# A decoder step bound by TensorE: a new opening for its first two units, side work moved between stages, and one group of heads fewer in plain form

## Chip, cores and metric

The kernel runs on one core of a Trainium2 chip. The metric is device microseconds of one execution. A core has five engines that run side by side, each in the order of its own queue: TensorE (PE; matmuls, with its weight loads shown as PEld), VectorE (DVE), ScalarE (ACT), GpSimd (POOL) and SyncE (SP). Here SP issues the loads and some stores, POOL issues most of the stores. Data lie in a fast memory of 128 partitions; matmuls write to a small second one (PSUM), and large arrays lie in DRAM.

## What is computed

One inference step of a two-layer decoder, on 1024 prompt tokens and 8 single decoded tokens, at width 2048, in float32:

```python
def pool_layer(x, prefix, pos, w_in, w_grp, scale, w_out, g_ln, b_ln):
    z = x @ w_in                                   # 2048 -> 4096: u and a gate
    u, gate = z[..., :D_POOL], z[..., D_POOL:]
    d, new_state = multiscale_pool(u, prefix, pos) # trailing means over 2, 4, 8, 16 tokens, minus u
    d = einsum('btgc,gce->btge', d, w_grp) * scale # four groups of 512 channels
    y = (d * silu(gate)) @ w_out
    return layer_norm(ALPHA * x + y, g_ln, b_ln), new_state

def shared_kv(h, pos, w_kv): ...                   # 4 key/value heads of 64, keys rotated

def attn_layer(x, pos, kb, vb, ...):
    z = x @ w_in                                   # 32 query heads of 64 (rotated) and a gate
    o = attn_core(q, kb, vb, q_pos, k_pos, sinks)  # causal window of 128, a learned sink per head
    y = (o * silu(gate)) @ w_out
    return layer_norm(ALPHA * x + y, g_ln, b_ln)
```

The first layer is `pool_layer`, then the keys and values are projected once, and the second layer is `attn_layer`. The outputs are both token streams and the new states and caches.

## The kernel before

Activations lie with channels on the partitions and tokens along the free axis. The tokens are worked in two chunks, 0 with 512 tokens and 1 with 520 (512 and the 8 decoded ones). The phases (PHASES, L50) follow each other in this order: `ai` (input projection, means, gate and group product of the first layer) for chunk 0 and then 1, `ao` (output projection and residual; its layer norm follows as side work) for 0 and 1, `bi` (keys, values, queries, gate and attention of the second layer) for 0 and 1, `bo` (its output projection) for 0 and 1.

**Products in float32 from three passes.** Each operand is split into a high part, a cast to the matmul's reduced format (on ScalarE: L502 for weights, L792 for activations), and a low part, the rest (a subtraction on DVE: L517 and L801). A product is three matmuls: high by high, high by low, low by high. So every piece of weights of 512 KB, once loaded, costs a cast and a subtraction before TensorE can use it up.

**Plain and Strassen form.** Most phases use a Strassen scheme of seven products (`seven`, L593): two output tiles of 128 channels at half the tokens, seven products of 8 x 3 = 24 matmuls with 256 or 260 columns (L681 to L683). The scheme needs sums of weight blocks and of activation blocks. Sums of weights are made by `first_pair` (L333, additions at L347) where a pair of tiles is used first, and may be stored for chunk 1, which loads them through `next_pair` (L319). Sums of activations, four per pair of rows, are made by `t_ops` (L843 to L853) and stored to DRAM as `Td`. The first part of `ai` chunk 0 and the first part of `bi` chunk 0 run in plain form (PLAIN, L57): there a tile of 128 output channels is a `unit` (L695) of two half steps with 24 matmuls of 512 columns each (L709 to L711). In `bi` chunk 0 the plain part has the keys and values (four units) and the first three pairs of query and gate tiles; a pair is four units, two with queries and two with gates. A pair takes two query tiles and so four heads.

**Order of work.** Every engine runs in the order of the source (L83). A counter `i` goes up at each `end()` (L541): once for each Strassen product, four times for each plain unit. Work that hangs on a product is put on this counter with `self.at(n, ...)`, n ends later. `begin()` (L529) loads the weights some pieces ahead, makes their casts and low parts three or four ahead and hands out the next piece. Beside this stand generators of side work (layer norms in `ln_gen`, L935; sums for the next phase in `t_gen`, L856; sums of weights in `sum_gen`, L428). `end()` takes one step of the first generator each time `i` passes a multiple of `every`, if at least `room` buffers are free (L554). `ready` (L570) runs a generator to its end at once if the next phase's input still hangs on it. Buffers come from one pool of 54 (`Mem`, L137), oldest freed first; a buffer whose last reader or store isn't done makes the new user wait.

**The start** (`start`, L2131). It issues, in turn, a load of the first weights (512 KB), eight loads of activation tiles (512 KB each, two rows of 128 channels by 512 tokens), with two more weight loads between them, and three small tables. Then come the casts and low parts in the order of need. The first unit uses all eight activation tiles one after the other; the next three units of the phase use them again. Four DVE groups (`t_first`, L748), placed at ends 3, 5, 7 and 9, make activation sums for the Strassen part.

**The means** (`pool_tile` and `pool_tail`, L1038 to L1105). After each unit ScalarE copies the result out (L1190); one end later DVE adds shifted copies (L1064), scales (L1085), and one end after that `rest` splits the result: a cast on ScalarE and the low part on DVE (`split`, L270 to L272) at the same end.

**Side work around the attention.** During `ao` chunk 1 the layer norm of chunk 0 runs, with `every` 2 and no sums for the Strassen part (its last argument is None, L2212). During the plain part of `bi` chunk 0, with `every` 1, run the layer norm of chunk 1 (with its sums), then `t_gen` for chunk 0, which loads the normalised rows again, makes the sums and stores them; ten additional steps are placed at ends 3, 5, ..., 21 (L2223). Beside them `sum_gen("wob")` may begin parts from end 4 to end 12. After a plain query unit the rotation (L1679, L1787) is put four ends after the unit's result is out, and TensorE's scores (L1817) one end later.

Of the kernel before, what the change touches and what calls it, by code (L numbers as in the profile page):

```python
# [9 lines left out]
F32 = mybir.dt.float32  # L10
# [37 lines left out]
N_CST = K_MP + P + 1  # L48

PHASES = (  # L50
    ("ai", 0, (0, 1)), ("ai", 0, (1, 8)), ("ai", 1, (0, 8)), ("ao", 0, None), ("ao", 1, None), ("bi", 0, (0, 3)),
    ("bi", 0, (3, 8)), ("bi", 1, (0, 8)), ("bo", 0, None), ("bo", 1, None),
)
PHASE_OF = {"x": "ai", "g": "ao", "h": "bi", "o": "bo"}
INPUT_OF = {k: x for x, k in PHASE_OF.items()}
# [133 lines left out]
class Kern:  # L189
# [185 lines left out]
    def build_stream(self):  # L375
        io = self.io
        w = []
        for kind, c, part in PHASES:
# [4 lines left out]
            if kind == "ai":  # L383
                for n in range(*part):
                    g, gates = divmod(n, 2)
                    for q in (8 * gates + 2 * g, 8 * gates + 2 * g + 1):
                        if n:
                            w += pr("wia", q)
                        elif c == 0:
                            w += self.bare_pair("wia", q)  # L390
                        else:
                            f = self.first_pair("wia", q, False)
                            w += [f[i] for i in ORDER7]
                    for h in range(2 if gates else 0):
                        w.append(self.lone(io["wg"][g][:, h * 1024 : (h + 1) * 1024]))
# [299 lines left out]
    def unit(self, done):  # L695
# [3 lines left out]
        for par in range(2):  # L699
            w = self.begin()  # L700
            wh, wl = (s.r for s in w)
            for k in range(8):
# [16 lines left out]
                if k in (3, 7):  # L719
                    self.end()  # L720


    def x_begin(self, n):

# [351 lines left out]
    def pool_tail(self, c, i, g, w, U, s, T, ext, dd, bufs, Us, work, add):  # L1076
        nc = self.nc
        for x in work:
            add(*x)
        if c == 0:  # L1080
            o = K_MP + g * NST
            nc.vector.tensor_mul(
                s[:, NST : NST + w - 1], s[:, NST : NST + w - 1], self.cst[:, o : o + w - 1]
            )
        nc.vector.scalar_tensor_tensor(  # L1085
            s[:, NST : NST + TP], s[:, NST : NST + TP], 1.0 / w, U[:, NST : NST + TP],
            op0=ALU.mult, op1=ALU.subtract,
        )
# [83 lines left out]
    def phase_ai(self, c, parts, nxt):  # L1172
# [5 lines left out]
        def means(g, end):  # L1178
            ext = es = None
            if T > TP:  # L1180
                es = self.mem.half(T)
                ext = es.a[:, :512].rearrange("p (i b w) -> p i b w", i=4, b=NDEC)
                nc.sync.dma_start(ext, io["st"][:, 4 * g : 4 * g + 4])
            dd = self.dd = {}
            for i in range(4):
                if not self.strassen:

                    def done(ps, i=i):
                        U = self.mem.full(NST + T)
                        nc.scalar.copy(U.a[:, NST : NST + T], ps[:])  # L1190
# [940 lines left out]
    def start(self):  # L2131
# [8 lines left out]
        self.load_to(1)  # L2140
        for n in range(8):
            self.x_load()
            if n in (3, 5):
                self.load_to(n // 2 + 1)
# [3 lines left out]
        self.prep_to(1)  # L2148
        for n in range(8):
            self.x_make()  # L2150
            if n == 3:
                self.prep_to(2)
# [7 lines left out]
    def run(self):  # L2160
# [15 lines left out]
        for n, (kind, c, part) in enumerate(PHASES):  # L2176
# [212 lines left out]
```

## Time and profile before

| | us |
|---|---|
| median of 3 runs | 2325.74 |
| lowest and highest | 2324.58, 2327.02 |
| the profiled execution | 2326.46 |
| its span, first to last instruction | 2324.7 |
| TensorE busy | 2290.2 |
| VectorE busy | 1935.0 |
| ScalarE busy | 1381.8 |
| GpSimd busy | 191.7 |

The times are those of whole executions; the profile shows one of them, and times in it count from the span's start. A row of the view of groups gives the line, the engine, the operation, output and input tiles with their shape, a count, then busy time, mean duration in ns, and the idle time of the engine just before with what ended it. A row of the timeline gives start, duration, and in brackets the idle time before it and its releaser. A row of the view of waits reads: who waited, for whom, total us, times, longest. A row of windows gives a stretch, its length, the busy time (and instructions) of PE, PEld, DVE, ACT and POOL, the clock that the throttle granted, the mean busy share of the 16 DMA engines, and GB/s. Matmuls and DVE operations overlap their neighbours, so the distance between two starts is less than a duration.

### The profile page before, as it was taken

The numbers are of one execution on the slowest core, as the hardware profiler recorded it, in microseconds if no ns is written. First come the engines' busy times: TensorE is split into PE (matmuls) and PEld (weight loads), VectorE is DVE, ScalarE is ACT, GpSimd is POOL, SyncE is SP. The second block draws the span as 40 slices with busy tenths as digits, with TensorE's granted clock in tenths as the row PEclk, the third lists the DMA queues.
The fourth block names the chain that finished last, engine by engine and source line by source line (L and its number), as shares of the span: only waits on it lengthen the run. The fifth ranks groups of instructions, "written<-read, shape, count | busy, mean of one in ns | idle before, by whom it ended". The sixth has DMA issues, their size and how long they took to land. (4 is left out here: it accounts for less than half of the span.)

```text
span 2324.7 us, 50174 instructions
## 1 busy us (share of the span) xinstructions
PE 2290.2 (99%) x20248; PEld 2208.9 (95%) x20248; DVE 1935.0 (83%) x2398; ACT 1381.8 (59%) x2531; POOL 191.7 (8%) x360
## 2 busy tenths in 40 slices
PE   8999999999999999999999999999999999999997
PEld 6999999999999999999778999999999999999997
DVE  7888889877878878878987888988987777898897
ACT  5554446544546556655466676785676678656565
POOL 0111110010000000000110111100000000000001
PEclk9999999999999999999999999999999999999999
DMA  6868679988889989898797667788586778799794
GB/s 247 280 252 304 234 243 333 322 299 302 303 306 317 338 284 336 321 350 310 236 349 256 220 224 254 256 306 259 178 262 225 252 233 284 254 368 363 266 345 157
DMA packets 247417, 652.50 MB, mean 281 GB/s; under 512 B 25328, under 2 KB 106128, under 8 KB 247184
## 3 DMA queue, kind: packets, MB, share of 16 engines
q1 hardware_dynamic: 205168, 496.81, 63.6%
q0 software_dynamic: 42016, 152.49, 17.0%
q8 instruction: 158, 2.59, 0.4%
q14 instruction: 75, 0.61, 0.1%
HBM read 466.68 MB, written 173.01 MB: 275 GB/s over the span
## 5 line engine op out<-in xcount | busy, mean ns | idle before, releaser
L681 PE MATMUL pD<-m,m 128*128 128x260 f32 (+1 forms) x4976 | 1408.7, 283 | 3.0 <-ACT pD L620 1.3
L683 PE MATMUL pD<-m,m 128*128 128x260 f32 (+1 forms) x4976 | 1402.2, 282 | 6.1 <-DVE m L517 5.7
L682 PE MATMUL pD<-m,m 128*128 128x260 f32 (+1 forms) x4976 | 1402.3, 282 | 0.0
L681 PEld LDWEIGHTS pD<-m,m 128*128 128x128 f32 x4976 | 936.6, 188 | 12.4 <-issue 6.0
L683 PEld LDWEIGHTS pD<-m,m 128*128 128x128 f32 x4976 | 937.7, 188 | 9.2 <-DVE m L517 9.2
L682 PEld LDWEIGHTS pD<-m,m 128*128 128x128 f32 x4976 | 937.0, 188 | 0.5
L517 DVE TENSOR_TENSOR m<-m,m 128x1024 fp32r<-128x1024 f32 x686 | 829.5, 1219 | 93.8 <-ACT m L502 53.8
L502 ACT CAST m<-m 128x1024 fp32r<-128x1024 f32 x686 | 716.9, 1050 | 237.7 <-DVE m L347 116.4
L347 DVE TENSOR_TENSOR m<-m,m 128x1024 f32<-128x1024 f32 x128 | 156.5, 1222 | 8.0 <-DMA m<-in_wia 3.8
L801 DVE TENSOR_TENSOR m<-m,m 128x1024 fp32r<-128x1024 f32 (+1 forms) x120 | 146.3, 1225 | 8.2 <-ACT m L792 4.0
L709 PE MATMUL pD<-m,m 128*128 128x512 f32 x320 | 128.7, 402 | 8.1 <-ACT m L792 8.1
L792 ACT CAST m<-m 128x1024 fp32r<-128x1024 f32 (+1 forms) x120 | 125.5, 1053 | 15.4 <-DVE m L517 4.8
L710 PE MATMUL pD<-m,m 128*128 128x512 f32 x320 | 127.2, 398 | 0.5 <-DVE m L801 0.5
L711 PE MATMUL pD<-m,m 128*128 128x512 f32 x320 | 126.8, 396 | 0.0
L654 ACT COPY m<-pD 128x260 f32<-128x260 f32 (+1 forms) x87 | 32.6, 374 | 128.8 <-PE pD L683 128.6
L642 DVE TENSOR_TENSOR m<-pD,m 128x260 f32<-128x260 f32 (+1 forms) x90 | 37.7, 419 | 76.7 <-ACT pD L641 70.8
L1853 ACT ACTIVATE m<-m,sm 128x128 f32<-128x128 f32 x256 | 99.8, 394 | 0.0
L1128 PE MATMUL pD<-m,m 128*128 128x260 f32 (+1 forms) x528 | 91.2, 323 | 0.0
L620 ACT ACTIVATE pD<-pD 128x260 f32<-128x260 f32 (+1 forms) x88 | 32.7, 371 | 98.3 <-PE pD L683 98.0
L1866 ACT ACTIVATE m<-m,sm 128x128 f32<-128x128 f32 x256 | 82.2, 394 | 12.2 <-DVE sm L1861 11.7
L1128 PEld LDWEIGHTS pD<-m,m 128*128 128x128 f32 x528 | 79.3, 188 | 8.0
L709 PEld LDWEIGHTS pD<-m,m 128*128 128x128 f32 x320 | 60.8, 190 | 23.4 <-ACT m L792 8.1
(247 smaller groups left out, 2065.0 us busy)
## 6 DMA issues: line engine op xcount, KB each, us to landing
m<-in_wia SPq DMA_DIRECT2D x130, 512.0 KB
m<-in_wib SPq DMA_DIRECT2D x130, 512.0 KB
m<-swoa SPq DMA_DIRECT2D x64, 512.0 KB
swia<-m POOLq DMA_DIRECT2D x56, 512.0 KB, 4.9
m<-swia SPq DMA_DIRECT2D x56, 512.0 KB
m<-swob SPq DMA_DIRECT2D x56, 512.0 KB
m<-in_wob SPq DMA_DIRECT2D x52, 512.0 KB
m<-in_woa SPq DMA_DIRECT2D x48, 512.0 KB
```

Source lines behind the costliest of these rows:

```text
L347: self.nc.vector.tensor_add(s[out].a[:, :1024], s[x].a[:, :1024], s[y].a[:, :1024])
L502: self.nc.scalar.copy(hi.r[:, :1024], self.stream[self.cast].src().a[:, :1024])
L517: self.nc.vector.tensor_sub(lo.r[:, :1024], s.src().a[:, :1024], hi.a[:, :1024])
L681: nc.tensor.matmul(ps[:, :TH], wh[:, s], h, start=new and k == 0, stop=False, skip_group_check=on)
L682: nc.tensor.matmul(ps[:, :TH], wh[:, s], l, start=False, stop=False, skip_group_check=on)
L683: nc.tensor.matmul(ps[:, :TH], wl[:, s], h, start=False, stop=k == 7, skip_group_check=on)
L709: nc.tensor.matmul(ps[:], wh[:, s], h, start=par == 0 and k == 0, stop=False)
L710: nc.tensor.matmul(ps[:], wh[:, s], l, start=False, stop=False)
L711: nc.tensor.matmul(ps[:], wl[:, s], h, start=False, stop=par == 1 and k == 7)
L792: self.nc.scalar.copy(h.r[:, :n], s.a[:, :n])
L801: self.nc.vector.tensor_sub(l.r[:, :n], s.a[:, :n], h.a[:, :n])
L1128: nc.tensor.matmul(ps[:, : cs.stop - cs.start], ws[:, s], d[:, cs], start=f0 and k == 0, stop=l0 and k == 3,)
```

## The change

Four things are changed.

1. **The start.** Seventeen products on zeros (256 columns) are put in front. The first two weight pieces and the first two activation tiles are loaded in halves of 256 KB, cast and split by halves (a and b are the weights, x and y the activations; None in the plan is a whole tile). A new function, `first_units`, runs the first two units side by side, each pair of activation rows being used for both before the next; eight more products on zeros stand between the first real ones. The order of the four weight pieces of these units is changed to match.
2. **Means of chunk 0.** The low part on DVE is put one end after the cast on ScalarE, and unit 2's means start two ends later.
3. **Two plain pairs.** The plain part of `bi` chunk 0 has pairs 0 and 1, not 0 to 2. Their weight sums aren't made in chunk 0, and are made in chunk 1 without being stored; pair 2's are made and stored in chunk 0's Strassen part.
4. **Side work.** The layer norm of chunk 0 in `ao` chunk 1 also makes the Strassen sums and has `every` 1.5; `t_gen` for chunk 0 is gone. In the plain part of `bi` chunk 0 there are fourteen additional steps at ends 5, 7, ..., 31, side work no longer waits for free buffers, and `sum_gen("wob")` may begin parts only from end 4 to end 5.

```diff
@@ PHASES and constants @@
-    ("ai", 0, (0, 1)), ("ai", 0, (1, 8)), ("ai", 1, (0, 8)), ("ao", 0, None), ("ao", 1, None), ("bi", 0, (0, 3)),
-    ("bi", 0, (3, 8)), ("bi", 1, (0, 8)), ("bo", 0, None), ("bo", 1, None),
+    ("ai", 0, (0, 1)), ("ai", 0, (1, 8)), ("ai", 1, (0, 8)), ("ao", 0, None), ("ao", 1, None), ("bi", 0, (0, 2)),
+    ("bi", 0, (2, 8)), ("bi", 1, (0, 8)), ("bo", 0, None), ("bo", 1, None),
-FORM = (1, 2,)
+FORM = (0, 1)
+WARM = 17
+FILL = 4, 1, 1, 1, 1
@@ build_stream @@
-                            w += self.bare_pair("wia", q)
+                            e = self.bare_pair("wia", q)
+                            w += [e[0], e[2], e[1], e[3]] if q == 0 else e
@@ new functions @@
+    def idle(self, n):
+        z = self.zero
+        for _ in range(n):
+            self.nc.tensor.matmul(self.zps[:, :256], z.r[:, :P], z.r[:, P:384], start=True, stop=True)
+
+    def first_units(self, dones):
+        nc = self.nc
+        banks = [self.psD() for _ in dones]
+        for par in range(2):
+            ws = {}
+            for n, (u, j) in enumerate((u, j) for j in range(4) for u in range(2)):
+                if u not in ws:
+                    ws[u] = self.begin()
+                elif n % 2 == 0:
+                    self.flush()
+                wh, wl = (a.r for a in ws[u])
+                x = self.x_get((par, j))
+                for i in range(2):
+                    k = 2 * j + i
+                    s = slice(k * P, (k + 1) * P)
+                    h, l = (a.rv(2, TP)[:, i, :] for a in x)
+                    nc.tensor.matmul(banks[u][:], wh[:, s], h, start=par == 0 and k == 0, stop=False)
+                    if par == 0 and n == 0:
+                        self.idle(FILL[i])
+                    nc.tensor.matmul(banks[u][:], wh[:, s], l, start=False, stop=False)
+                    nc.tensor.matmul(banks[u][:], wl[:, s], h, start=False, stop=par == 1 and k == 7)
+                if par == 0 and n < 3:
+                    self.idle(FILL[2 + n])
...
+                if n % 2:
+                    self.end()
@@ pool_tail, rest @@
-            self.split(*hl, s[:, NST : NST + T])
-            for b in bufs + [Us]:
-                b.free()
+            nc.scalar.copy(hl[0], s[:, NST : NST + T])
             dd[i] = (*hl, d)
+            def low():
+                nc.vector.tensor_sub(hl[1], s[:, NST : NST + T], hl[0].bitcast(F32))
+                for b in bufs + [Us]:
+                    b.free()
+            low() if c else self.at(1, low)
@@ phase_ai, means @@
-                        self.at(1, lambda: self.pool_tile(c, 4 * g + i, U, None, dd))
+                        self.at(3 if i == 1 else 1, lambda: self.pool_tile(c, 4 * g + i, U, None, dd))
-                    self.unit(done)
+                    if i < 2:
+                        twins.append(done)
+                        if i:
+                            self.first_units(twins)
+                    else:
+                        self.unit(done)
@@ start @@
+        z = self.zero = self.mem.full()
+        nc.vector.memset(z.a[:, :384], 0.0)
+        self.zps = self.psD()
+        self.idle(WARM)
+        plan = [
+            ("a", 0, 512), ("x", 0, TP), ("x", TP, 2 * TP), ("b", 0, 512), ("y", 0, TP), ("y", TP, 2 * TP),
+            ("a", 512, 1024), None, ("b", 512, 1024), None,
+        ]
+        for it in plan:
+            if it is None:
+                self.x_load()
+                continue
+            k, lo, hi = it
+            if k in "ab":
+                nc.sync.dma_start(raw[k].a[:, lo:hi], {"a": qa, "b": qb}[k][:, lo:hi])
+            else:
+                nc.sync.dma_start(raw[k].a[:, lo:hi], src["xy".index(k)][:, lo // TP, :])
+        self.loaded = 2
+        for n in range(4, 8):
+            if n in (4, 5):
+                self.load_to(n - 1)
+            self.x_load()
+        self.load_to(5)
...
+            h, l = both[k]
+            nc.scalar.copy(h.r[:, lo:hi], raw[k].a[:, lo:hi])
+            nc.vector.tensor_sub(l.r[:, lo:hi], raw[k].a[:, lo:hi], h.a[:, lo:hi])
...
+        for n in range(4, 8):
+            if n in (4, 5):
+                self.prep_to(n - 1)
             self.x_make()
@@ run @@
             elif (kind, c) == ("ao", 1):
-                gen = self.ln_gen(0, *acc[0], C_GA, C_BA, self.act["h", 0], None)
+                gen = self.ln_gen(0, *acc[0], C_GA, C_BA, self.act["h", 0], self.Td["h", 0])
-                self.every = 2
+                self.every = 1.5
             elif (kind, c) == ("bi", 0) and not self.strassen:
-                for k in (4, 12):
+                for k in (4, 5):
                     self.at(k, lambda k=k: setattr(self, "on", k == 4))
-                add(("h", 0, False), self.t_gen(("h", 0)))
-                for k in range(10):
-                    self.at(2 * k + 3, lambda: self.side and self.lastO < self.i - 1 and self.side_step())
-                self.every = 1
+                for k in range(14):
+                    self.at(2 * k + 5, lambda: self.side and self.lastO < self.i - 1 and self.side_step())
+                self.every, self.room = 1, -20
```

More of the change, by code (lines that the diff above doesn't have):

```diff
@@ L719, in unit @@
                 if k in (3, 7):
+                    self.end()
[26 more added lines that the diff above has]
+                    self.idle(FILL[2 + n])
+                if par == 0 and n == 3:
+                    self.zero.free()
+                if u == 1:
+                    self.x_used((par, j))
+                if n == 7:
+                    for w in ws.values():
+                        for a in w:
+                            a.free()
+                    if par == 1:
+                        self.posts += [lambda ps=ps, done=done: done(ps) for ps, done in zip(banks, dones)]
+                if n % 2:
                     self.end()
@@ L1184, in means @@
             dd = self.dd = {}
+            twins = []
             for i in range(4):
@@ L2139, in start @@
         nc.scalar.copy(self.jr[:], self.area[:, :P])
-        self.load_to(1)
-        for n in range(8):
+        z = self.zero = self.mem.full()
+        nc.vector.memset(z.a[:, :384], 0.0)
+        self.zps = self.psD()
+        self.idle(WARM)
+        qa, _, qb, _ = self.quads("wia", 0)
+        src = [self.act["x", 0][:, 4 * j : 4 * j + 4 : 2, :] for j in range(2)]
+        raw = {k: self.mem.full() for k in "abxy"}
+        both = {k: (self.mem.full(), self.mem.full()) for k in "abxy"}
+        plan = [
+            ("a", 0, 512), ("x", 0, TP), ("x", TP, 2 * TP), ("b", 0, 512), ("y", 0, TP), ("y", TP, 2 * TP),
+            ("a", 512, 1024), None, ("b", 512, 1024), None,
+        ]
+        self.xl = self.xl[2:]
+        for it in plan:
[11 more added lines that the diff above has]
+                self.load_to(n - 1)
             self.x_load()
-            if n in (3, 5):
-                self.load_to(n // 2 + 1)
+        self.load_to(5)
         nc.sync.dma_start(self.prm[:], io["prm"])
@@ L2147, in start @@
         nc.sync.dma_start(self.cst[:, K_MP : K_MP + 4 * NST], io["rc"])
-        self.prep_to(1)
-        for n in range(8):
+        self.hl[0], self.hl[1] = both["a"], both["b"]
+        self.cast = self.made = self.prepped = 2
+        for n, k in enumerate("xy"):
+            self.x0[0, n], self.xnew[0, n] = raw[k], both[k]
+        self.xq = self.xq[2:]
+        for it in plan:
+            if it is None:
+                self.x_make()
+                continue
+            k, lo, hi = it
+            h, l = both[k]
+            nc.scalar.copy(h.r[:, lo:hi], raw[k].a[:, lo:hi])
+            nc.vector.tensor_sub(l.r[:, lo:hi], raw[k].a[:, lo:hi], h.a[:, lo:hi])
+        for k in "ab":
+            raw[k].free()
+        for n in range(4, 8):
+            if n in (4, 5):
+                self.prep_to(n - 1)
             self.x_make()
-            if n == 3:
-                self.prep_to(2)
         for j in range(4):
```

## The prediction

> **What bounds the kernel now.** I read the page's first lines, then TensorE's waits, then the engines in order of time where the change touches them.
>
> ```profile
> span 2324.7 us, 50174 instructions
> PE 2290.2 (99%) x20248; PEld 2208.9 (95%) x20248; DVE 1935.0 (83%) x2398; ACT 1381.8 (59%) x2531; POOL 191.7 (8%) x360
> ```
> ```profile
> PE pD L709 <- ACT m L792: 8.1, 1, 8.1
> PE pD L683 <- DVE m L517: 5.7, 9, 1.3
> PE pS L1817 <- DVE m L1787: 2.2, 2, 1.5
> ```
>
> TensorE is busy for all but 34.5 us of the span. So only two things pay: fewer or faster columns through TensorE, or the removal of one of its few waits. The longest wait is the start (8.1 us); the others are short, and nearly all on VectorE (DVE). DVE's mean of 83% hides stretches near 100%, so DVE is what can take a gain back. The start in order of time:
>
> ```profile
> 5.31 1.05 ACT L502 CAST m<-m 128x1024 fp32r<-128x1024 f32 x1 [2.98 <-DMA m<-in_wia]
> 6.96 1.05 ACT L792 CAST m<-m 128x1024 fp32r<-128x1024 f32 x1 [0.60 <-DMA m<-in_x]
> 8.06 0.80 PE L709 MATMUL pD<-m,m 128*128 128x512 f32 x1 [8.06 <-ACT m L792]
> 8.34 1.05 ACT L792 CAST m<-m 128x1024 fp32r<-128x1024 f32 x1 [0.34 <-DMA m<-in_x]
> 9.32 0.80 PE L710 MATMUL pD<-m,m 128*128 128x512 f32 x1 [0.46 <-DVE m L801]
> 9.91 0.63 PE L711 MATMUL pD<-m,m 128*128 128x512 f32 x1
> 14.18 0.63 PE L709 MATMUL pD<-m,m 128*128 128x512 f32 x1
> 15.29 0.39 PE L709 MATMUL pD<-m,m 128*128 128x512 f32 x1
> 34.00 0.39 PE L709 MATMUL pD<-m,m 128*128 128x512 f32 x1
> 55.99 0.39 PE L711 MATMUL pD<-m,m 128*128 128x512 f32 x1
> ```
>
> The second column is a matmul's latency; its cost is the distance between starts. Ten starts from 9.91 to 14.18 stand 0.427 apart; 176 from 15.29 to 55.99 stand 0.231 apart. TensorE thus begins at about half speed for 7 us. Matmul 97, the first of unit 3, starts at 34.00.
>
> **Part 1, the start.** Before, the first product needs two whole 512 KB pieces. What the DMA had moved by when:
>
> ```profile
> 0.00:3.10 3.10, 0.00 (x0) 0.00 (x0) 0.00 (x0) 1.58 (x2) 0.46 (x6) 1.00 0.37 86
> 0.00:4.15 4.15, 0.00 (x0) 0.00 (x0) 0.00 (x0) 1.58 (x2) 0.46 (x6) 1.00 0.50 124
> 0.00:5.97 5.97, 0.00 (x0) 0.00 (x0) 0.00 (x0) 2.24 (x3) 0.46 (x6) 1.00 0.62 176
> ```
> ```profile
> 31.48 0.62 ACT L271 CAST m<-m 128x512 fp32r<-128x512 f32 x1 [5.71 <-DVE m L1085]
> 32.50 0.68 DVE L272 TENSOR_TENSOR m<-m,m 128x512 fp32r<-128x512 f32 x1
> L782 SPq DMA_DIRECT2D m<-in_x x8: 368/458/806, 1.2 to 8.3; - x8
> ```
>
> GB/s times length gives 267 KB by 3.10, 515 KB by 4.15, 1051 KB by 5.97. The casts waiting for 524 KB and 1049 KB began at 5.31 and 6.96, 1.0 to 1.15 after those bytes. Pieces of 262 KB should then land near 4.2, 5.2, 6.2, 7.0, 7.6, 8.3 and 9.0 in the plan's order (first weights, two x, second weights, two x, first weights' rest), since the bytes flow in the same order. SP issues six DMAs more, but at 0.46 each (median) the first eight are out before 5, ahead of the bytes. A half cast takes 0.62, a half low part 0.68. The first product can start at 5.2 + 0.65 = 5.85, against 8.06. Its low parts come at 6.5 and 7.5, the second unit's weights at 8.25, the next x at 9.6. Each pair of x tiles now feeds twelve products (2.8 us) and not six, so TensorE waits for data until about 9.6, with 12 products done; the remaining 84 of the two units take 84 x 0.231 = 19.4, and some 0.9 goes to fillers and small waits. Unit 3 starts near 29.9: **4.1 us earlier**.
>
> The 17 products on zeros (256 columns, 0.213 each at the slow rate, 3.6 us) run from about 1.2 to 4.8 (DVE's memset of 384 columns is a fraction of the 0.9 us of its 128x1024 memset). They lie inside the wait for the first piece, so cost nothing; without that cover they would cost 3.6. The eight fillers (1.7 slow, 0.9 fast) lie in the waits for low parts. Bounds: no piece lands earlier and the slow rate stays, 1 us gained; nothing late after 5.85, 5 us.
>
> That gain must survive DVE, which is full when unit 4 ends:
>
> ```profile
> 19.06 1.05 ACT L792 CAST m<-m 128x1024 fp32r<-128x1024 f32 x1 [0.36 <-DMA m<-in_x]
> 21.37 2.35 DVE L517 TENSOR_TENSOR m<-m,m 128x1024 fp32r<-128x1024 f32 x2
> 45.00:53.00 8.00, 8.00 (x37) 6.51 (x36) 5.24 (x7) 5.34 (x8) 1.90 (x4) 1.00 0.58 193
> 53.00:75.00 22.00, 20.19 (x155) 19.16 (x154) 21.90 (x23) 16.38 (x22) 0.53 (x1) 1.00 0.62 203
> 46.03 0.69 DVE L1064 TENSOR_TENSOR m<-m 128x512 f32<-128x512 f32 x1 [1.11 <-ACT m L1190]
> 52.80 0.69 DVE L272 TENSOR_TENSOR m<-m,m 128x512 fp32r<-128x512 f32 x1 [1.64 <-ACT m L271]
> 68.83 0.39 PE L683 MATMUL pD<-m,m 128*128 128x256 f32 x1 [0.90 <-DVE m L517]
> ```
>
> From 53 to 75 DVE has 0.1 us free and TensorE waits 1.8. DVE has only two idle spots behind it, 1.1 (TensorE's unit 3 late) and 1.64 (the low part waiting for a cast that stands behind another on ScalarE). The first goes with the earlier unit, the second is what the later low part removes: that DVE instruction is issued a step later, with nothing waiting. DVE also leads by a little: the last x tile, cast at 19.06 as the eleventh whole piece, now comes twelfth, one piece (1.38) later, so its low part ends near 20.4 + 1.05 + 1.23 = 22.7; but by then four weight tiles are done too, which before took until 23.7 (the row at 21.37). Lead 1.0. Together 1.0 + 1.1 + 1.64 = 3.8; TensorE's 4.1 is capped there. I take **-3.8** (range -1 to -5).
>
> **Part 2, two plain pairs of heads instead of three.**
>
> ```profile
> L709 PE MATMUL pD<-m,m x256: 387/393/588, 1076.5 to 1276.0; 128*128 128x512 f32 x128
> 125.00:175.00 50.00, 50.00 (x426) 1.00 0.64 231
> ```
>
> L709 is one third of a unit's products: 256 are 16 units of 48. The pair leaving the plain stage has 4 units, 192 products of 512 columns: 192 x 0.231 = 44.4. Its Strassen form is 2 x 7 x 24 = 336 products of 256 columns at 50/426 = 0.117: 39.4. **-5.0**; scores, transposes and values of its heads are paid in either form.
>
> It adds six weight tiles (cast and low part) and the small evictions. The eight sums of weights move from chunk 1 to chunk 0, and pair 0's from the plain stage to chunk 1. DVE has room for a pair in the Strassen stage, where one pair now takes:
>
> ```profile
> 1321.00:1368.00 47.00, 47.00 (x521) 46.10 (x521) 43.63 (x51) 32.41 (x77) 6.53 (x13) 1.00 0.69 241
> ```
>
> That is 93% with no wait of TensorE. Nothing to pay as long as it holds; bound 0 to 4 if it doesn't.
>
> **Part 3, side work.** The four sums per row pair of the attention input move from a generator in the plain stage into chunk 0's layer norm, at one step in 1.5 products, not 2.
>
> ```profile
> 960.00:1007.00 47.00, 46.77 (x391) 46.56 (x390) 46.48 (x44) 31.49 (x46) 1.07 (x2) 1.00 0.98 360
> 1007.00:1045.00 38.00, 38.00 (x320) 38.00 (x319) 22.41 (x22) 17.03 (x26) 1.07 (x2) 1.00 0.96 348
> L1023 DVE TENSOR_TENSOR m<-m,m 128x1040 f32<-128x1040 f32 x8 | 9.8, 1234 | 0.0
> L852 DVE TENSOR_TENSOR m<-m,m 128x260 f32<-128x260 f32 x8 | 3.4, 430 | 0.3
> ```
>
> In the first row chunk 0's last loop runs, in the second it is done. (The lower two rows are chunk 1's, from 1140 to 1192: one product with the deviation, and the last of the four sums.) DVE gets 32 sums of 0.43 more, 14 us, against 15.6 free in the second row. Two steps in 3 products carry 2.5 + 1.7 of DVE work where one step in 2 carried 2.5: 1.4 against 1.25 per product. The DMA gets eight stores (4.2 MB) more over a longer loop at the same rate, and eight loads less later. SP's queue gets nothing new, POOL's eight issues. Full but not over: I take **+0.3** (0 to 2).
>
> In the plain stage the second chunk's layer norm must now fit into 12 units:
>
> ```profile
> 1140.00:1192.00 52.00, 50.54 (x336) 40.51 (x335) 51.28 (x77) 35.57 (x76) 8.64 (x17) 1.00 0.92 332
> L289 DVE TENSOR_TENSOR m<-m,m 128x1024 f32<-128x1024 f32 x8 | 9.8, 1221 | 0.1
> 1177.88 1.32 PE L1817 MATMUL pS<-m,m 64*32 64x160 f32 x64 [1.46 <-DVE m L1787]
> ```
>
> The norm's last loop is 9.8 + 4 x 3.4 = 23.4 of the 51.3. At 1.5 steps a half unit instead of about one it takes 37 us instead of 52, but the 9.8 of pair 0's sums are gone: (51.3 - 9.8 - 23.4)/52 + 23.4/37 = 98%, against 99%. The score at 1177.88 waits because the rotation (L1787) stands in DVE's queue behind that work; before it in the queue stood all eight sums and most of the loop, now the loop alone, some 2 us less. I take **-1.0** (-1.5 to 0 in this case).
>
> Sum: -3.8 - 5.0 - 1.0 + 0.3 = **-9.5**. The profiled execution took 2326.46 (span 2324.7 and 1.8 around it), 0.7 above the median of 2325.74; against that median: **2316.2**.
>
> **Rivals.** *DVE keeps the start's gain*: only DVE's lead of 1.0 reaches the Strassen stage and TensorE waits longer at 68. For: 21.9 of 22.0 busy. Against: both idle spots have a cause that the change removes. 2319.0.
>
> *The slow rate lasts*: full speed came 5 us after the steady run at 9.91 began. If the pause from 4.8 to 5.85 spoils the zeros' run, it comes near 11 again; the second unit's first six products then take 2.6 and not 1.4, and those to 11 lose 0.3 or more: 1.5 lost, part 1 is -2.6: 2317.4. Against: 3.6 us of products come before the pause. The Trainium skill, "TensorE: Matmul & The Clock Gate", Part 1, has the clock halved until a free-running window of about 3.4 us is full of activity; the trace agrees on the halving, not on the length. By that rule the zeros need not fill one window.
>
> *Small pieces are slow*: if each half piece cost as much time as a whole one (1.38 from the cast at 6.96 to that at 8.34), eight would add 8 x 0.69 = 5.5 and the start gains nothing: 2320. The Trainium skill, "DMA: Bandwidth & Descriptors", Rules for kernel authors, asks for 1 MiB or more per DMA, which speaks for this. The trace speaks against it: the x tiles already move in runs of 2 KB, the half pieces' size, and land at the pace of the bytes.
>
> *The pair isn't worth 5*: TensorE waits for low parts in the added pair, DVE being at 93%. 2320 to 2322, say 2321.
>
> *Slower*: the second chunk's norm is no longer held back by free buffers, so in the plain stage a buffer it takes may still be read by a store:
>
> ```profile
> p<-m POOLq DMA_DIRECT2D x12, 520.0 KB, 5.6
> ```
>
> DVE then stands still for up to 5.6, with rotations and low parts queued behind and a score waiting for each; one half unit (2.8) is slack. Eight passes at 2.8 are 22 us: 2339. It decides from four passes (9.5/2.8). For: DMA at 0.92, DVE full. Against: DVE stands idle for only 0.7 of those 52 us now.
>
> **How the numbers follow.** Forecast 0.52; DVE keeps the gain 0.14; slow rate 0.10; small pieces 0.06; pair not worth it 0.10; slower 0.08. About 0.2% (4.7 us) is what a measurement tells from no change: faster means under 2321.1. The first four and a third of the fifth lie there: 0.85; the rest of the fifth makes 0.07 the same; 0.08 slower. The range goes from all upper gains (-5 - 5 - 1.5, and 1.8 of TensorE's other waits: 2312.4) to the end of the fifth case, leaving out the slower one and tails: 2312.4 to 2322.
>
> **What would show it.** Right: first real product near 5.9, distances of 0.23 before 10, unit 3 near 29.9, no DVE idle near 52; the plain stage some 44 plus its small share of attention shorter; no score wait over 1; 336 more products of 256 columns. Wrong: first product after 6.9; waits on L517 over 3 us at the Strassen stage's start; DVE idle on DMA among L985, L1023 and L849 to L852 in the plain stage; new waits around 960 to 1045.

## The result, and the profile after

The changed kernel takes 2322.32 us (median of 21 runs, 2320.17 to 2325.46) against 2325.79 for the kernel before (21 runs, 2323.02 to 2328.41): ratio 0.9985, 95% interval 0.9979 to 0.9991. That is 3.5 us faster; 9.5 were forecast, and the time lies just above the range (2322.0). The profiled execution of the changed kernel is the fastest of its 21, 2320.17, so the two profiles differ by 6.3.

The page's first lines and TensorE's waits, after:

```profile
span 2317.9 us, 50529 instructions
PE 2288.1 (99%) x20417; PEld 2217.7 (96%) x20417; DVE 1943.0 (84%) x2409; ACT 1389.3 (60%) x2548; POOL 191.1 (8%) x360
```
```profile
PE pD L686 <- DVE m L520: 4.9, 9, 0.9
PE pD L672 <- ACT m L657: 4.9, 1, 4.9
```

The 8.1 us of the start have gone from this view (1.3 are left, ahead of the products on zeros), and one new wait of 4.9 stands in it. (Lines have moved: L517 is now L520, L654 is L657, L669 is L672, L681 to L683 are L684 to L686, L782 is L828, L1671 is L1728, L1787 is L1844, L1817 is L1874.) The start, in order of time:

```profile
1.32 4.00 PE L730 MATMUL pD<-m 128*128 128x256 f32 x17 [1.32 <-DVE m L2198]
5.33 0.50 PE L749 MATMUL pD<-m,m 128*128 128x512 f32 x1
9.32 0.39 PE L752 MATMUL pD<-m,m 128*128 128x512 f32 x1
9.55 0.39 PE L753 MATMUL pD<-m,m 128*128 128x512 f32 x1
29.65 0.40 PE L712 MATMUL pD<-m,m 128*128 128x512 f32 x1
51.60 0.40 PE L714 MATMUL pD<-m,m 128*128 128x512 f32 x1
```

First real product at 5.33 (forecast 5.85), distances of 0.23 by 9, unit 3 at 29.65 (29.9), last plain product at 51.60 instead of 55.99: 4.4 earlier. The start did what was forecast. To see where that went, I took the start of each stage from the timelines (the stages differ in columns: 512, 256, 260). First row: the kernel before, in us; below it, how much earlier (minus) other profiles get there. The e-rows belong to the experiments below. Each row is one execution; that of e1 is the slowest of its 11.

| | first product | ai 0, Strassen | ai 1 | ao 1 | bi 0, plain | last product of bi 0 | bi 1, second group of 24 | bo 0 | bo 1 | last product |
|---|---|---|---|---|---|---|---|---|---|---|
| before | 8.1 | 56.2 | 383.9 | 913.1 | 1076.5 | 1516.6 | 1521.6 | 1958.0 | 2132.7 | 2302.5 |
| after | -2.7 | -4.4 | -3.9 | -3.9 | -3.7 | **-10.2** | **-3.2** | -5.5 | -5.1 | -6.7 |
| e1 | -2.8 | -4.0 | -4.4 | -4.4 | -4.3 | -3.1 | +1.6 | -0.3 | +2.4 | +2.0 |
| e2 | 0.0 | -0.3 | -0.1 | -0.3 | -0.1 | -5.7 | -5.3 | -9.1 | -7.5 | -8.3 |
| e3 | -2.6 | -4.2 | -3.6 | -3.7 | -3.3 | -10.1 | -8.8 | -11.6 | -10.7 | -12.6 |
| e6 | -2.8 | -3.7 | -3.9 | -3.9 | -3.8 | -10.3 | -6.9 | -8.1 | -6.8 | -8.9 |
| e7 | -2.7 | -4.2 | +0.5 | -0.1 | 0.0 | -6.8 | -6.5 | -2.9 | -2.1 | -3.2 |
| e8 | -2.6 | -4.3 | -4.3 | -4.2 | -4.2 | +13.5 | +14.6 | +13.4 | +12.9 | +11.8 |

The row "after" says it: 4 us from the start, 6.5 more across `bi` chunk 0, 10.2 in all when that stage ends. Up to there the forecast sum holds. By the second 24 products of chunk 1, 7.0 of them are gone. That place in the timelines, before and then after:

```profile
1516.63 0.28 PE L683 MATMUL pD<-m,m 128*128 128x256 f32 x1
1517.37 0.62 PE L669 MATMUL pD<-m,m 128*128 128x260 f32 x3 [0.46 <-ACT m L654]
1517.84 0.37 PE L681 MATMUL pD<-m,m 128*128 128x260 f32 x1
1518.04 0.28 PE L682 MATMUL pD<-m,m 128*128 128x260 f32 x1
1518.16 0.28 PE L683 MATMUL pD<-m,m 128*128 128x260 f32 x1
```
```profile
1506.40 0.28 PE L686 MATMUL pD<-m,m 128*128 128x256 f32 x1
1511.60 1.02 PE L672 MATMUL pD<-m,m 128*128 128x260 f32 x3 [4.92 <-ACT m L657]
1512.41 0.42 PE L684 MATMUL pD<-m,m 128*128 128x260 f32 x1
1512.63 0.42 PE L685 MATMUL pD<-m,m 128*128 128x260 f32 x1
```

TensorE stands for 4.92 us, and behind the pause its products are 0.217 apart where they were 0.118. The windows view shows why (the third number from the end is the granted clock), again of after:

```profile
1500.00:1525.00 25.00, 20.08 (x193) 19.49 (x179) 19.03 (x25) 19.89 (x45) 0.86 (x2) 0.86 1.04 380
1511.60:1517.50 5.90, 5.90 (x27) 5.90 (x28) 3.28 (x3) 4.57 (x12) 0.00 (x0) 0.50 1.05 389
```

The clock is halved there. 24 products at 0.217 cost 24 x 0.099 = 2.4, the three in front 0.3 (0.81 instead of 0.47 from the first of them to the next line). With 4.92 - 0.46 = 4.5 of pause, **7.2 of the 10.2 us are lost at this one place**, as the table has it (7.0).

What is late? TensorE waits for an eviction on ScalarE (L657), and ScalarE has the same instructions in the same order as before. It stood still for 2.66 and 3.49 us shortly ahead:

```profile
1497.28 1.06 ACT L838 CAST m<-m 128x1040 fp32r<-128x1040 f32 x1 [2.66 <-DMA m<-h]
1504.33 1.05 ACT L505 CAST m<-m 128x1024 fp32r<-128x1024 f32 x1 [3.49 <-DVE m L1960]
```

The cast at 1497.28 waits for a load of h. Loads are SP's, so I read SP's queue there, before and then after:

```profile
1491.29 1.95 SPq L782 DMA_DIRECT2D m<-h  x2
1493.33 3.71 SPq L1671 DMA_DIRECT2D m<-m  x4
1497.15 0.80 SPq L283 DMA_DIRECT2D m<-in_wkv  x1
```
```profile
1480.71 0.38 SPq L828 DMA_DIRECT2D m<-h  x1
1487.73 0.38 SPq L828 DMA_DIRECT2D m<-th  x1
1488.20 3.11 SPq L1728 DMA_DIRECT2D m<-m  x4
1491.41 1.15 SPq L828 DMA_DIRECT2D m<-h  x1
1492.73 0.59 SPq L285 DMA_DIRECT2D m<-in_wkv  x1
```

Before: two loads of h, four partner copies of the last rotation (`m<-m`), weights of the keys. After: a load of th (the sums for Strassen) stands ahead of the copies, and it goes out only at 1487.73, 7 us behind the load ahead of it. The view of SP's waits names what it waited for, and the view by tile the store itself (after, both):

```profile
SPq L828 <- DMA o<-m: 6.4, 1, 6.4
```
```profile
L1963 POOL DMA_DIRECT2D o<-m x1: 547/547/547, 1481.1 to 1481.1; - x1
DMA to landing us min/median/max: 6.5/6.5/6.5
```

The th load's buffer was still being read by a store of an attention result, issued at 1481.1 and done 6.5 later. In the source this load comes after the copies. What I wrote ahead of the prediction, that every engine runs in the order of the source, is wrong for SP: L83 holds PE, DVE and ACT to it, while the build may put SP's loads in another order (178 of the changed kernel's 915 stand behind one that comes later in the source). In the kernel before, the first load of th there comes at 1501.60, after the copies, and no load of h or th in that stretch waits for a store.

**Theory (hoist)**: this one load, ahead of its turn and held by a store, delays what is behind it by 4 to 5 us (the copies come 18.2 us ahead of the stage's last product, before 23.3), and that is the pause and the low clock. **Rivals**: *outrun*, ScalarE and DVE are the bound at the change of chunks and take back any lead; *third*, the pause belongs to this one profile.

### The profile page after: what moved, and what is told of

Same layout as the page of the kernel before. It is cut to its first block, busy times and chain, and to the rows that moved or that the text cites. A ratio compares the mean times of both kernels' runs of the same rounds, so it can differ in the third digit from the quotient of the medians.

```text
span 2317.9 us, 50529 instructions
## 1 busy us (share of the span) xinstructions
PE 2288.1 (99%) x20417; PEld 2217.7 (96%) x20417; DVE 1943.0 (84%) x2409; ACT 1389.3 (60%) x2548; POOL 191.1 (8%) x360
## 5 line engine op out<-in xcount | busy, mean ns | idle before, releaser
L684 PE MATMUL pD<-m,m 128*128 128x260 f32 (+1 forms) x5088 | 1441.3, 283 | 4.7 <-ACT pD L623 2.3
L686 PE MATMUL pD<-m,m 128*128 128x260 f32 (+1 forms) x5088 | 1434.7, 282 | 4.9 <-DVE m L520 4.9
L685 PE MATMUL pD<-m,m 128*128 128x260 f32 (+1 forms) x5088 | 1434.7, 282 | 0.0
L684 PEld LDWEIGHTS pD<-m,m 128*128 128x128 f32 x5088 | 959.4, 189 | 13.9 <-issue 6.2
L686 PEld LDWEIGHTS pD<-m,m 128*128 128x128 f32 x5088 | 959.8, 189 | 7.1 <-DVE m L520 7.0
L520 DVE TENSOR_TENSOR m<-m,m 128x1024 fp32r<-128x1024 f32 x690 | 833.5, 1218 | 94.7 <-ACT m L505 44.1
L349 DVE TENSOR_TENSOR m<-m,m 128x1024 f32<-128x1024 f32 x136 | 166.1, 1222 | 10.2 <-DMA m<-in_wia 5.7
L838 ACT CAST m<-m 128x1024 fp32r<-128x1024 f32 (+1 forms) x118 | 123.3, 1051 | 11.8 <-DVE m L520 3.5
L657 ACT COPY m<-pD 128x260 f32<-128x260 f32 (+1 forms) x89 | 33.2, 373 | 131.0 <-PE pD L686 131.0
L1179 PE MATMUL pD<-m,m 128*128 128x260 f32 (+1 forms) x528 | 91.5, 323 | 0.0
L712 PE MATMUL pD<-m,m 128*128 128x512 f32 x224 | 89.1, 398 | 0.0
L714 PE MATMUL pD<-m,m 128*128 128x512 f32 x224 | 88.2, 394 | 0.0
L713 PE MATMUL pD<-m,m 128*128 128x512 f32 x224 | 88.1, 393 | 0.0
L632 ACT COPY m<-pD 128x260 f32<-128x260 f32 (+1 forms) x92 | 34.3, 373 | 82.3 <-PE pD L686 82.0
```

What stands on the lines that cost most here:

```text
L349: self.nc.vector.tensor_add(s[out].a[:, :1024], s[x].a[:, :1024], s[y].a[:, :1024])
L520: self.nc.vector.tensor_sub(lo.r[:, :1024], s.src().a[:, :1024], hi.a[:, :1024])
L684: nc.tensor.matmul(ps[:, :TH], wh[:, s], h, start=new and k == 0, stop=False, skip_group_check=on)
L685: nc.tensor.matmul(ps[:, :TH], wh[:, s], l, start=False, stop=False, skip_group_check=on)
L686: nc.tensor.matmul(ps[:, :TH], wl[:, s], h, start=False, stop=k == 7, skip_group_check=on)
L712: nc.tensor.matmul(ps[:], wh[:, s], h, start=par == 0 and k == 0, stop=False)
```

## The experiments

Each was timed against the kernel before on the same chip, in five rounds.

**e1 and e2: the change in two halves.** e1 has the start and the means (PHASES, FORM and `run` as before), e2 the two pairs and the side work (start, means and order of the first weights as before).

```diff
e1: -FORM = (0, 1)       +FORM = (1, 2,)     (and ("bi", 0, (0, 3)), ("bi", 0, (3, 8)), run() as before)
e2: -FORM = (1, 2,)      +FORM = (0, 1)      (and ("bi", 0, (0, 2)), ("bi", 0, (2, 8)), run() as changed)
```

> Parts 1 alone: the kernel before with the new start and the later low parts; three plain groups, FORM and side work as in the kernel before. Hoist theory (a th load stands ahead of the partner copies in SP's order at the end of chunk 0's attention stage, and waits some 6 us for an output store; what is behind it on SP is late): here SP's list has the th load hoisted too (h, th, partner copies), so the stage ends some 4 us earlier than before's 1516.9, TensorE then pauses 3 to 6 us at the first product of chunk 1, the granted clock of that stretch falls under 0.95, and of the 4 us at most 1 is left, down to 3 us slower: 2325 to 2329 against 2325.8. Outrun theory (ScalarE is the bound at the chunk change, whatever SP's order, so that any lead is given back there): 2325 to 2327, with a pause of about 4, just what was gained. Third theory (the start's gain does not repeat from run to run, and the chunk change only happened once): 2325.8 within 1 with no pause there.

> Parts 2 and 3 alone: the kernel before with two plain groups, FORM (0, 1) and the new side work; start and means as before. Hoist theory: here SP's list keeps the order of before (h, h, partner copies, wkv, h, h, wkv, th), so there is no pause over 1.5 us at the chunk change, and the sum of the parts holds: 6 us faster, 2318.5 to 2321.5. Outrun theory: the lead of about 6 is given back at the chunk change, a pause of 4 to 6 there and a lower clock behind it, 2324 to 2327. Third theory: as the sum, 2320.

e1: 2326.39 (ratio 0.9999, 0.999 to 1.0007). e2: 2319.91 (0.9974, 0.9964 to 0.9984). In e1's SP queue the th load stands ahead of the copies again, and TensorE's waits and the stretch show the pause; in e2 they don't. e1, then e2:

```profile
PE pD L672 <- ACT m L657: 3.8, 1, 3.8
1500.00:1525.00 25.00, 21.25 (x235) 20.48 (x235) 19.70 (x23) 19.90 (x44) 0.86 (x2) 0.93 1.04 375
```
```profile
PE pD L669 <- ACT m L654: 1.0, 1, 1.0
1500.00:1525.00 25.00, 24.02 (x285) 22.95 (x285) 23.22 (x28) 22.84 (x49) 0.85 (x2) 1.00 1.05 385
```

So the start alone brings nothing that can be told from noise in the end, though it is 4 us ahead as far as the plain stage and 3 at the change of chunks; the pairs bring their 6 with no pause, against *outrun*, which wanted it there too. The hoisted load comes with the start and the means, since e1 has it and e2 hasn't. That their buffers move the rotation of the pool, and so the build's order, is the likely way, but no run shows it.

**e3, e4 and the control e10: SP's order pinned.** From the last group of `bi` chunk 0 to 14 products into chunk 1, SP is held to the source's order as well; in the changed kernel (e3), in e1 (e4) and in the kernel before (e10).

```diff
-    for i in tc.nc.cur_bb.bb.instructions:
-        if i.engine in ENGINES:
+    for n, i in enumerate(tc.nc.cur_bb.bb.instructions):
+        if i.engine in ENGINES or i.engine == mybir.EngineType.SP and any(a <= n < b for a, b in marks):
```

> The changed kernel with one thing pinned: from the last group of chunk 0's attention stage to 14 products into chunk 1's, SP issues in the order of the source (partner copies, h, h, wkv, h, h, wkv, th). Nothing else in SP's list moves but two weight loads behind it. Hoist theory: the pause of 4.9 shrinks to under 1.5, the clock there stays over 0.97, and the time is 9 to 10.5 under that of the kernel before: 2315.3 to 2317. Outrun theory: the pause stays at 3 to 5, since ScalarE has the same instructions in the same order, and the time is 2320 to 2323. Third theory (pause of that one profile): as the changed kernel, 2322.

> e1 with SP's order pinned in the same stretch. Hoist theory: no pause over 1.5, and the start's 4 us arrive at the end: 2321 to 2323, that is 3 to 5 under the kernel before and 3 to 8 under e1. Outrun theory: as e1, 2325 to 2327.

> The control: the kernel before with the same stretch of SP's list in the order of the source. There no load stood ahead that had to wait for a store; the partner copies go two loads earlier, and a few weight loads later on change places. Hoist theory: no more than 1 us either way, 2324.8 to 2326.8. Rival (source order in this stretch is good for several us whatever the kernel, so e3's gain isn't the removal of something that the change brought): 2319 to 2323.

e3: 2315.16 (0.9952, 0.994 to 0.9965). e4: 2321.99 (0.9982, 0.9973 to 0.9991). e10: 2326.09 (1.0, 0.9992 to 1.0009). SP's queue and TensorE in e3:

```profile
1483.12 3.33 SPq L1728 DMA_DIRECT2D m<-m  x4
1486.55 1.14 SPq L828 DMA_DIRECT2D m<-h  x2
```
```profile
1508.56 0.63 PE L672 MATMUL pD<-m,m 128*128 128x260 f32 x3 [1.72 <-ACT m L657]
```

The copies go out 5 us earlier, the pause falls from 4.92 to 1.72 (a little more than expected), and with not one instruction less the kernel is about 7 us faster. The start's 4 us arrive (e4), the sum of all parts arrives (e3), and pinning brings nothing where nothing was hoisted (e10). *Outrun* and *third* fall. e3 is faster than both kernels.

**e5: the pause filled.** The data stay late, but TensorE works through most of the pause:

```diff
+        if c == 0:
+            t = self.psd[2].tile([P, 512], F32, tag="D", name=self.nm("pD"))
+            for _ in range(44):
+                nc.tensor.matmul(t[:, :P], self.jr[:], self.jr[:], start=True, stop=True)
```

> The changed kernel, its hoisted load left as it is, with 44 matmuls of 128 columns on a constant put behind the last product of chunk 0's attention stage: they fill part of TensorE's pause of 4.9 us and write nothing that is read. The data reach TensorE as late as before. If the lowered clock behind the pause (granted clock 0.86 in the stretch from 1500 to 1525, products 0.217 apart for 6 us where they were 0.118) comes from the pause, the clock there is over 0.97, the products stand at 0.118, and 2 to 3 us come back: 2319.3 to 2320.5. Rival (the clock falls for another reason, or the late data cost the same whether TensorE pauses or not): 2322 to 2323.

2318.6 against 2327.37 on this chip (0.9968, 0.9955 to 0.998), so by the ratios some 4 us faster than the changed kernel. Windows, then the timeline of e5:

```profile
1500.00:1525.00 25.00, 24.74 (x278) 24.00 (x277) 20.68 (x25) 22.20 (x47) 0.86 (x2) 1.00 1.05 388
```
```profile
1507.05 5.03 PE L2188 MATMUL pD<-jr 128*128 128x128 f32 x44
1512.33 0.62 PE L672 MATMUL pD<-m,m 128*128 128x260 f32 x3 [0.24 <-ACT m L657]
```

The clock stays at 1.00: it is the pause that halves it. The gain is above the 2.7 worked out from the one profile (the two profiles stand 1.8 apart at the second group of 24), but its interval reaches down to that.

**e11: which of the late issues counts.** The four copies go to POOL's queue; the th load stays where it is on SP.

```diff
-            self.nc.sync.dma_start(t.a[32 * a : 32 * a + 32, : n * T], s.a[32 * b : 32 * b + 32, : n * T])
+            q = self.nc.gpsimd if self.other else self.nc.sync      # other: last group of bi chunk 0
+            q.dma_start(t.a[32 * a : 32 * a + 32, : n * T], s.a[32 * b : 32 * b + 32, : n * T])
```

> The changed kernel with the hoisted load left where it is on SP; only the four partner copies of chunk 0's last group are issued by POOL, whose queue there is short. The copies then start some 5 us earlier, while the loads of h and of the keys' weights stay as late. If the late loads set the pause (ScalarE's waits of 2.66 for h and 3.49 in the changed kernel's profile), the pause stays at 3 to 5 and the time at 2320.5 to 2323. If the late copies set it (VectorE's wait of 1.46 for them, and all that stands behind the rotation), the pause is under 2 and the time 2315 to 2318.

2317.69 against 2326.43 (0.9968, 0.9957 to 0.9979). The copies are out at 1483.5, but the pause is still 3.9, with ScalarE waiting for the weights of the keys (e11):

```profile
1503.31 1.05 ACT L505 CAST m<-m 128x1024 fp32r<-128x1024 f32 x1 [3.41 <-DMA m<-in_wkv]
```

The late loads set most of the pause. (The wait of 3.49 that the changed kernel's profile puts down to L1960 is at the same cast, and by this profile a load.) The time is better than the 2320.5 to 2323 expected in that case all the same: the loads go out with four issues fewer ahead of them, and the clock is at 0.93 in that stretch, not 0.86.

**e6, e7 and e8: e3 with one piece taken back**, to price the terms of the sum.

```diff
e6: -WARM = 17; FILL = 4, 1, 1, 1, 1       +WARM = 0; FILL = 0, 0, 0, 0, 0
e7: -low() if c else self.at(1, low)       +low()      (and unit 2's means at 1, not 3)
e8: run() as in the kernel before, with the two plain pairs
```

> e3 without the products on zeros (none in front, none between). By the prediction's working the first products then run at about half speed until some 11 us: 3 us of TensorE's 4.1 are lost, 2317.5 to 2318.5 against e3's 2315.2, and the first real products stand 0.4 apart. Rival (VectorE sets the pace of the first 75 us, so that TensorE's slow start costs little): 2315 to 2316.5.

> e3 with the low parts of chunk 0's means made at the same end as their cast, and unit 2's means one end after the unit, as in the kernel before. By the prediction the low part waits for its cast again (1.64 us of idle VectorE near 50) and the start's gain is cut by that: 2316.3 to 2317.2 against e3's 2315.2. Rival (VectorE has slack there after the new start): 2315.2 within 0.5.

> e3 with the side work of the kernel before (chunk 0's layer norm without sums and every 2, the generator t_gen in the plain stage, ten additional steps, sums of the last projection's weights from end 4 to 12, five buffers kept free), in a plain stage of two groups. By the prediction part 3 is worth 0.7: 2315.5 to 2317 against 2315.2. Rival (the shorter plain stage can't hold the old side work, so that ready() runs the rest at once and TensorE waits): 2319 to 2325, with waits over 2 us on VectorE or on the input at the end of the plain stage.

e6: 2317.55 against 2327.37 (0.9953, 0.9939 to 0.9967), the same as e3. The products do run at half speed until 10.87:

```profile
5.28 0.79 PE L749 MATMUL pD<-m,m 128*128 128x512 f32 x1 [5.28 <-ACT m L2241]
10.44 0.60 PE L753 MATMUL pD<-m,m 128*128 128x512 f32 x1
10.87 0.41 PE L749 MATMUL pD<-m,m 128*128 128x512 f32 x1
```

yet the twelfth product starts at 10.44, only 0.9 later than in the changed kernel (9.55), and the Strassen stage only 0.5 later than in e3: slow products fill the time in which fast ones wait for the next pieces, with fillers between. In the profiles the zeros cost nothing and are worth 0.5 there, and nothing by chunk 1 (-3.9 against -3.6); so the gain lies in the rest of the new start, the loads in halves and each x used for two units.

e7: 2324.25 (0.9991, 0.9982 to 1.0), 8 us worse than e3. As forecast the idle DVE is back, to the hundredth:

```profile
51.24 0.69 DVE L1150 TENSOR_TENSOR m<-m,m 128x512 fp32r<-128x512 f32 x1 [1.64 <-ACT m L1146]
```
```profile
67.27 0.58 PE L686 MATMUL pD<-m,m 128*128 128x256 f32 x1 [1.89 <-DVE m L520]
50.00:75.00 25.00, 22.14 (x161) 21.05 (x160) 23.65 (x25) 18.83 (x25) 1.50 (x3) 0.93 0.59 197
```

but its price isn't 1.6. TensorE's wait at 67 grows to 1.89 (0.74 in e3) and the clock drops behind it, a wait near 355 grows to 2.12 (0.82), and by chunk 1 e7 is 4.1 us behind e3 (table: +0.5 against -3.6). At the second group of `bi` chunk 1 it is 2.3 behind, at `bo` 0 8.7: the larger part of its loss lies in `bi` chunk 1, with waits of up to 2.9. SP's list differs from e3's in many places there, which I didn't separate, so the 8 us are not the price of the later low part.

e8: 2340.98 (1.0065, 1.0053 to 1.0078), 26 us worse than e3. Its plain stage, TensorE's waits and DVE's stretch ahead of the first of them:

```profile
PE pD L714 <- DVE m L520: 13.1, 1, 13.1
PE pS L1874 <- ACT m L1989: 6.1, 1, 6.1
1153.00:1180.00 27.00, 13.93 (x61) 10.97 (x59) 26.45 (x65) 10.75 (x27) 7.77 (x15) 0.83 1.02 403
```

DVE does almost nothing but norm and sums for 27 us: when the next phase's input is asked for, `ready` runs all that is left in one go. The new side work is worth far more than 0.7: with the old one, a plain stage of two pairs costs 26 us.

**e9: SP's whole list in source order.**

```diff
-ENGINES = (mybir.EngineType.PE, mybir.EngineType.DVE, mybir.EngineType.Activation)
+ENGINES = (mybir.EngineType.PE, mybir.EngineType.DVE, mybir.EngineType.Activation, mybir.EngineType.SP)
```

> The changed kernel with SP's whole list in the order of the source (178 of its 915 loads stood behind a later one, 9 now). If the order of issue matters only where a hoisted load meets a long store, as at the end of chunk 0's attention stage, this is worth what e3 is: 2314 to 2317 on a chip where the kernel before takes 2325.8. If other hoisted loads cost as well, it is under 2312. Rival: elsewhere the hoisting helps, since a load whose buffer is free goes ahead of one that has to wait; then in strict order new waits on casts appear and it is 2318 to 2330, with e3's gain at the chunk change kept.

2314.84 against 2325.97 (0.9955, 0.9942 to 0.9969): as e3. Taken together, the other hoisted loads neither cost nor gain; single ones may, against each other.

## Why the prediction was wrong

- **Part 1, -3.8: right.** 34.00 - 29.65 = 4.35 at unit 3 (4.1 forecast), of which 3.7 to 3.9 are left from chunk 1 on; 3.9 by e4's medians. Within it "the slow rate lasts" was given 1.5 us; e6 has the slow rate and loses 0.5. The later low part (with unit 2's later means) holds DVE's side of it open, as said, but its absence costs 4.1 by chunk 1 and not 1.6 (e7 against e3).
- **Part 2 and the plain stage's side work, -5.0 - 1.0: right in sum.** 6.5 us from the start of the plain stage to the end of `bi` 0, 5.6 in e2, whose whole gain is 5.9; no run separates the two terms. (The prediction's "half unit (2.8)" is a quarter of a unit: 48 products take 11.1.) No score waits over 1: TensorE's waits have 0.2 in all where they had 2.2.

```profile
PE pS L1874 <- DVE m L1844: 0.2, 1, 0.2
```

- **Part 3 in `ao` chunk 1, +0.3: not contradicted**, 0.2 by the table, which is too small to tell from noise; no wait of TensorE where the row of before in the prediction has 0.23:

```profile
960.00:1007.00 47.00, 47.00 (x395) 47.00 (x394) 44.05 (x55) 27.36 (x40) 3.70 (x7) 1.00 0.99 370
```

- **The step that failed** is the last, "Sum: -3.8 - 5.0 - 1.0 + 0.3 = -9.5". It takes each gain to the end. The prediction has "SP's queue gets nothing new" for part 3, and for part 1 no word on SP's order behind the first loads, so it puts the late cost of part 1 at nothing without a reason. SP did get a new *order* (e1). Over 1400 us behind part 1, with no line of the diff near, a load is sorted ahead of its turn onto a buffer that a store still reads, and 7.2 us go in pause and low clock. Taken away in e3, the sum comes out: 2315.16 - 2325.84 = -10.7 (ratio 0.9952, 0.994 to 0.9965) against -9.5.
- **The rivals.** "Slower" had the mechanism, a buffer still read by a store and a queue standing behind it, with the store's landing time for its price (5.6 there, 6.5 here); but I looked for it on DVE in the plain stage, where the change touched the buffers, and not on SP. "The pair isn't worth 5" came nearest in time (2321) and was wrong in substance.
- **Open**: the medians gain less than the profiles (3.5 us, and 6.3 between the profiled executions), and only one execution of the changed kernel has a trace. The mean granted clock of each is on record: its median is 0.996 over the changed kernel's 21, 0.997 in the profiled one and 0.998 in e3's five. So the others spent at least as long at the low clock; how long each paused isn't shown. Why the build sorts just this load forward is open too.

## What to carry to other kernels

A gain early in a kernel with a shared pool of buffers and a sorted load queue can be spent far from the edit: after a change, compare the time at which each stage begins, not only the totals, and where a lead vanishes compare the order of the load queue. A queue that issues in order turns one load whose buffer is still being stored into a delay of all behind it; forecast such a change with a term for it. And price a piece of support work by what happens without it (e8), not by the idle time that it removes.

## What the runs showed of the hardware

A pause of TensorE can cost more than its length. After 4.92 us the stretch of 25 us has a mean clock of 0.86, that is half speed for (1 - 0.86) x 25 x 2 = 7.0 us; after 3.8 it has 0.93, 3.5 us; after 1.72 (e3) none. In between the length doesn't decide: the clock fell after 1.89 (e7, above) and after 2.3 at the change of chunks in e6 (first row), and not after a pause of 2.9 in e7 that ends at 1696.75 (the other two):

```profile
1500.00:1525.00 25.00, 22.73 (x232) 21.94 (x215) 21.40 (x27) 22.10 (x48) 1.01 (x2) 0.93 1.05 384
```
```profile
1675.00:1700.00 25.00, 22.10 (x253) 21.29 (x253) 16.04 (x23) 14.88 (x38) 0.72 (x1) 1.00 0.70 214
1700.00:1725.00 25.00, 25.00 (x280) 24.44 (x279) 18.39 (x25) 17.86 (x45) 1.99 (x3) 1.00 0.81 261
```

By these traces, what decides is where the pause lies. The clock records in the traces give the moment of each change: in all 13 profiles the changes lie a whole number of steps of 3.413 us behind the first record (e6's two falls at the changes of chunk and stage, 1509.34 and 1949.65, are 129 steps apart). All 24 falls come at the end of a step in which TensorE was idle for 0.56 of it or more (the least is e7's, at 67.13). At 0.46 or less a full clock never fell, and the one step in between, 0.55 in e10 near its end, kept it too. (The idle shares are worked out from the matmuls' starts and modelled ends.) e7's pause of 2.9 lies across two steps, 0.42 and 0.43 of each. So whether a pause of about 2 us costs 1.7 more (half speed for 3.41) is a matter of when it comes.

The Trainium skill, "TensorE: Matmul & The Clock Gate", Part 1, has a free-running window of about 3.4 us behind this; the grid, and low stretches of one and two such lengths (3.41 in e6, 6.83 in the changed kernel), agree with it. It has the clock fall after at least one idle window; the pauses of 1.89 and 2.3 are shorter than that, so there the measurement decides.

At the start the windows view misleads: e6's products are 0.43 apart from 5.28 to 10.87 while it gives a granted clock of 1.00:

```profile
5.00:10.00 5.00, 4.72 (x10) 3.42 (x11) 3.68 (x6) 3.21 (x6) 0.00 (x0) 1.00 0.94 306
```

The trace's first clock record, of the full clock, stands at 10.88 in e6, at 5.36 in the changed kernel and at 15.07 in the kernel before; ahead of it the trace has none, and the view prints 1.00. The products on zeros thus bring the full clock 5.5 us earlier, though they are worth 0.5 us at most.
